# Hybrid attention and recurrence backbone on one core: row maxima over 96 rows, the recurrence's products in fp32, joint logarithms

## The chip, the cores and the metric

One core of one Trainium2 chip runs the whole program in one launch. The metric is device time in microseconds (us), the median of the runs. The engines are TensorE (PE, with its weight loads as PEld), VectorE (DVE), ScalarE (ACT), GpSimd (POOL) and SyncE (SP, which issues the transfers). Each engine takes its own instructions strictly in the order in which the program wrote them.

## The reference, cut to what matters

Two layers over 256 context and 512 latent tokens of width 1024. In each, one in-projection feeds four mixers of four heads (64 wide): A, differential attention; B, a gated recurrence in both directions (HGRN2); C, grouped-query attention; D, a 2-D Fourier transform. An out-projection and a SwiGLU block follow. The change is mostly in B and C:

```python
def forget_gate(z, lb):
    sig = jax.nn.sigmoid(z)
    log_f = jnp.log(lb + (1 - lb) * sig)
    key = (1 - lb) * jax.nn.sigmoid(-z)
    return log_f, key

# B: o_t = sum over s <= t of (q_t . k_s decayed by f between s and t) v_s,
#    forward and backward, latent tokens starting from the context's state
        decay = jnp.where(incl, jnp.exp(rel), 0.0)
        scores = jnp.einsum('bhtd,bhsd,bhtsd->bhts', qc, kc, decay)
        o_intra = jnp.einsum('bhts,bhse->bhte', scores, vc)

# C: 4 query heads on 2 key heads
def gqa_core(q, k, v):
    s = jnp.einsum('bqhgd,bkhd->bhgqk', q.astype(F32), k.astype(F32)) * HEAD_DIM ** -0.5
    p = jax.nn.softmax(s, axis=-1)
    return jnp.einsum('bhgqk,bkhd->bqhgd', p, v.astype(F32)).astype(v.dtype)
```

All inputs are fp32. In layer 0 the gate's lower bound `lb` is zero, so its logarithm has a short form there; layer 1 needs a second logarithm.

## The kernel before, in words

**Tiling.** Tokens are held in three groups g = 0 (context), 1 and 2 (latent), 256 tokens each. A projection multiplies fp16 halves in three passes (high by high, high by low, low by high) into fp32 PSUM; the latent stream's projections are the `MATMUL` lines L2014 and L2019, the FFN's are L2129 (three passes) and L2169, L2233. For most tiles the FFN's first product uses seven products of half-size sums in place of eight (`p_ffn_pair`, L2169); tiles listed in `TUNE['cl']` use plain passes (L2129).

**Order.** The program is written once by `Plan.run`, a list scheduler: each piece of work is a thread with a priority (`pr_...` in `TUNE`) that yields operations with an estimated cost on an engine, or on a choice of two. The plan always writes the operation that can start first by its own estimates. So any changed cost or priority reorders the whole program, and the order it writes is fixed on the chip.

**Mixer C.** `a_prep`/`c_prep` normalise, rotate and split q and k into fp16 halves. Keys are laid out as 192 rows of two tiles `kt[:, 0]` (128 rows) and `kt[:, 1]` (96 rows); `tr` fills them with transposes of 128 and of 64 columns (L1339, L1340). `c_att` first wants each query's largest score, before the score product itself: for each head j and key group it runs a 128-row product (L1376, high and low half of q) and a 64-row product (L1377, high half of q by low half of k), and takes the maximum over the two banks. The maximum then becomes two rows (64 and 65) of a 96-row tile `s2`, which holds the high half of q in rows 0 to 63; its transpose gives `qt[0:96, 1]`, and the score product (L1404, L1405: 128 rows, then 96) subtracts the maximum on the way. `score_thread` follows with exponentials (L1192) and their fp16 halves `ph` and `pl`, the latter by a DVE or POOL subtraction (L424), for A and C alike.

**Mixer B.** `b_gate` and `b_gates` turn gate columns into logarithms: per token group, three `Ln` (L1468) that need another ACT table than the `Exp` around them. `b_levels` forms the decayed scores by doubling: block widths 0, 1, 2, 4 up to 128, with a decay tile E at each (`b_decay`, products at L1605, L1638, L1674), then multiplies scores by values: `b_split` copies a score bank as fp16 high half and subtracts it for the low half (L1553, DVE), and `b_pv` runs `mm3`, three fp16 products of 64 columns (L1514), four times per bank. `b_v` makes the fp16 halves of the values, the low one at L1508. `b_join` does the pairs of latent groups 1 and 2 (fp32 products over 64 rows, L1774), one row half r of a head pair at a time; `b_state` and the products at L1804 bring in the context's state.

Two lines on which much rests:

```python
for n, (i, j) in enumerate(((0, 0), (0, 1), (1, 0))):
    T.matmul(o, lhsT=A[i], rhs=B[j], start=(start and n == 0), stop=(stop and n == 2), skip_group_check=True)
```

Of the kernel before, what the change touches and what calls it, by code (L numbers as in the profile page):

```python
# [97 lines left out]
class Plan:  # L98
# [5 lines left out]
    def __init__(self):  # L104
        self.eng = {}
# [180 lines left out]
def op(eng, cost, reads, writes, fn, port=False):  # L286
    return ("op", ((eng, cost, fn, 0.0, port),), reads, writes)
# [26 lines left out]
def c_act(n, ap=0):  # L314
    return 0.065 + n * 0.833e-3 + 0.093 * ap
# [16 lines left out]
def kernel(ctx: ExitStack, tc: tile.TileContext, xg, wall, wmod, pk32, pk16, dftx, dftc, out):  # L332
# [34 lines left out]
    nhalf = const.tile([128, 16], F32, name="nhalf")  # L367
    vA = [const.tile([128, 2, 4, 2, 65], F16, name=f"vA{g}") for g in range(NG)]
# [21 lines left out]
    st = {}  # L390
# [5 lines left out]
    def aop(cost, r, w, f):  # L396
        return op("act", cost, r, w, f)
# [277 lines left out]
    def prep_thread():  # L675
# [30 lines left out]
        for l in range(NL):  # L706
# [11 lines left out]
            yield vop(0.8, ["cst", "pk32b"], [("lam", l)], f2)  # L718
# [59 lines left out]
    def norm_thread(l, w, g):  # L778
# [1782 lines left out]
```

## Time and profile before

| what | value |
|---|---|
| median of 3 runs | 1769.31 us (1768.81 to 1769.59) |
| profiled execution, its own time | 1768.02 us |
| its span, first to last instruction | 1766.2 us |
| PE busy in the span | 1690.3 us, 96% |
| DVE busy | 1505.1 us, 85% |
| ACT busy | 999.1 us, 57% |
| POOL busy | 142.5 us, 8% |
| mean granted PE clock | 0.975 of full |

The profile is of one execution. A share of busy time is a mean over stages with different limits, so the stages are read apart: in-projection and mixers of layer 0 lie at about 100 to 521 us of the span, its FFN at 521 to 1030, the mixers of layer 1 at 1030 to 1408, its FFN at 1408 to 1766. A PE that is busy all through a stage sets its length; where PE has gaps and DVE has none, DVE does. Matmuls overlap, so the duration of one is not its price: the price is the distance between the starts of neighbours, and is read from the timeline.

### The profile page before, as it was taken

The numbers are of one execution on the slowest core, as the hardware profiler recorded it, in microseconds if no ns is written. First come the engines' busy times: TensorE is split into PE (matmuls) and PEld (weight loads), VectorE is DVE, ScalarE is ACT, GpSimd is POOL, SyncE is SP. The second block draws the span as 40 slices with busy tenths as digits, with TensorE's granted clock in tenths as the row PEclk, the third lists the DMA queues.
The fourth block names the chain that finished last, engine by engine and source line by source line (L and its number), as shares of the span: only waits on it lengthen the run. The fifth ranks groups of instructions, "written<-read, shape, count | busy, mean of one in ns | idle before, by whom it ended". The sixth has DMA issues, their size and how long they took to land. (4 is left out here: it accounts for less than half of the span.)

```text
span 1766.2 us, 46475 instructions
## 1 busy us (share of the span) xinstructions
PE 1690.3 (96%) x19913; PEld 1439.0 (81%) x19913; DVE 1505.1 (85%) x3182; ACT 999.1 (57%) x1816; POOL 142.5 (8%) x166
## 2 busy tenths in 40 slices
PE   8999988899999999999999999999779999999998
PEld 6687877577788889999899888868668888887887
DVE  6888799788569888899889997988999678888887
ACT  5647876465456554355435484539768555465454
POOL 0122021120000000000000002311011000000000
PEclk9999999699999999999999999999979999999999
DMA  9822010145234653521354151000124323452531
GB/s 375 319 83 85 26 57 27 49 132 204 73 132 133 213 170 112 182 81 59 119 179 129 44 180 49 26 25 18 34 73 145 107 83 105 126 185 79 178 122 49
DMA packets 62863, 201.47 MB, mean 114 GB/s; under 512 B 6848, under 2 KB 9152, under 8 KB 62656
## 3 DMA queue, kind: packets, MB, share of 16 engines
q1 hardware_dynamic: 62656, 198.50, 33.6%
q8 instruction: 156, 2.56, 0.6%
q14 instruction: 51, 0.42, 0.1%
HBM read 178.55 MB, written 19.92 MB: 112 GB/s over the span
## 5 line engine op out<-in xcount | busy, mean ns | idle before, releaser
L424 DVE TENSOR_TENSOR g<-g,g 128x512 f32<-128x512 f32 (+6 forms) x705 | 444.3, 654 | 60.5 <-ACT g L410 43.8
L412 ACT ACTIVATE g<-g 128x512 f16<-128x512 f32 (+2 forms) x397 | 243.8, 639 | 247.1 <-DVE g L424 244.6
L2169 PE MATMUL ps<-g,g 128*128 128x256 f16 (+1 forms) x4200 | 374.9, 251 | 0.1
L2169 PEld LDWEIGHTS <-g 128*128 128x128 f16 x4200 | 339.0, 98 | 39.3 <-issue 11.1
L428 DVE SCALAR_TENSOR_TENSOR g<-g,g 128x512 f16<-128x512 f32 (+4 forms) x450 | 305.3, 695 | 56.4 <-ACT g L412 53.2
L2014 PE MATMUL ps<-g,g 128*128 128x256 f16 x2256 | 272.2, 274 | 1.0 <-DVE g L428 1.0
L2233 PEld LDWEIGHTS <-g 128*128 128x128 f16 x2709 | 227.4, 98 | 36.6 <-issue 11.0
L2014 PEld LDWEIGHTS <-g 128*128 128x128 f16 x2256 | 219.0, 98 | 31.8 <-issue 1.7
L410 ACT CAST g<-g 128x512 f16<-128x512 f32 (+3 forms) x283 | 170.4, 613 | 111.6 <-DVE g L424 67.9
L2233 PE MATMUL ps<-g,g 128*128 128x256 f16 (+1 forms) x1917 | 214.4, 271 | 10.2 <-ACT g L410 3.7
L2019 PE MATMUL ps<-g,g 128*128 128x256 f16 x1632 | 197.8, 274 | 0.2 <-DVE g L424 0.2
L2019 PEld LDWEIGHTS <-g 128*128 128x128 f16 x1632 | 155.9, 98 | 28.9 <-issue 7.5
L2129 PE MATMUL ps<-g,g 128*128 128x256 f16 x1440 | 159.7, 273 | 0.0
L2129 PEld LDWEIGHTS <-g 128*128 128x128 f16 x1440 | 140.8, 98 | 17.3 <-issue 0.8
L410 ACT COPY g<-ps 128x512 f32<-128x512 f32 (+4 forms) x130 | 74.2, 572 | 114.2 <-PE ps L814 27.1
L1192 ACT ACTIVATE g<-ps 128x512 f32<-128x512 f32 x156 | 91.4, 597 | 32.4 <-PE ps L1226 22.4
L424 DVE TENSOR_TENSOR pl<-g,ph 128x512 f16<-128x512 f32 x130 | 88.7, 693 | 11.3 <-ACT ph L410 10.2
L424 DVE TENSOR_TENSOR g<-g 128x256 f32<-128x256 f32 (+3 forms) x203 | 93.7, 468 | 3.2 <-ACT g L748 1.8
L410 ACT CAST ph<-g 128x512 f16<-128x512 f32 (+2 forms) x149 | 84.9, 576 | 4.2 <-DVE g L424 1.4
L2427 PE MATMUL ps<-p16c 128*128 128x256 f16 x590 | 75.1, 282 | 3.8 <-DMA p16c<-in_pk_dram 3.8
L2427 PEld LDWEIGHTS <-p16c 128*128 128x128 f16 x590 | 58.9, 102 | 16.5 <-issue 4.2
L1212 PEld LDWEIGHTS <-ph 128*128 128x128 f16 x1248 | 65.4, 98 | 5.6 <-issue 3.2
(242 smaller groups left out, 2243.5 us busy)
## 6 DMA issues: line engine op xcount, KB each, us to landing
g<-in_wall_dram SPq DMA_DIRECT2D x180, 512.0 KB, 4.6
g<-in_wmod_dram SPq DMA_DIRECT2D x96, 512.0 KB, 6.6
g<-xsc SPq DMA_DIRECT2D x40, 256.0 KB, 4.9
xsc<-g SPq DMA_DIRECT2D x40, 256.0 KB, 3.0
g<-in_xg_dram SPq DMA_DIRECT2D x12, 512.0 KB, 6.9
g<-in_wall_dram SPq DMA_DIRECT2D x16, 384.0 KB, 3.3
xsc<-g SPq DMA_DIRECT2D x10, 512.0 KB, 2.8
g<-xsc SPq DMA_DIRECT2D x10, 512.0 KB, 5.4
```

What stands on the lines that cost most here:

```text
L410: S.copy(o, i)
L412: S.activation(out=o, in_=i, func=AF.Copy, scale=scale)
L424: return either(r, w, ("dve", c_dve(n), lambda: V.tensor_tensor(**f()), bias, True), ("pool", c_pool(n), lambda: G.tensor_tensor(**f()), 0 ...
L428: return vop(c_dve(n), r, w, lambda: V.scalar_tensor_tensor(**f()), True)
L1192: yield aop(c_act(512), [k], [k + (0,)], lambda pp=pp, bank=bank: S.activation(out=pp, in_=bank, func=AF.Exp, scale=scale))
L1212: T.matmul(bank[:, u, t, :], lhsT=a[:, i, q], rhs=v[:, b, :], start=(n == 0), stop=(n == 6 * nk - 1))
L2014: T.matmul(bank[:, cb, :], lhsT=W[a][:, kw, 128 * cb:128 * cb + 128], rhs=xh[b][:, kx, :], start=(first and n == 0), stop=(last and n == 2 ...
L2019: T.matmul(bank[:, t, :], lhsT=xh[b][:, k, 128 * t:128 * t + 128], rhs=wt[a][:, k, :], start=(first and n == 0), stop=(last and n == 2), s ...
L2129: T.matmul(bank[:, cb, :], lhsT=wt[a][:, k % 4, :], rhs=xh[b][:, k % 4, :], start=(k == 0 and n == 0), stop=(k == 7 and n == 2), skip_grou ...
L2169: T.matmul(into[name], lhsT=wt[:, y, kk, :], rhs=x[:, z, kk, :], start=(name in ("P1", "P6") and kk == 0 and n == 0), stop=(kk == 3 and n ...
L2233: T.matmul(o, lhsT=wt[:, y, j % 4, :], rhs=x[:, z], start=(name in ("P1", "P6") and j == js[0] and n == 0), stop=(j == js[-1] and n == 2), ...
L2427: T.matmul(t[:, 0:256], lhsT=ident16, rhs=p16[:, 128:384], start=True, stop=True)
```

## The change: what it does

1. **Row maxima of C.** The 64-row product becomes a 96-row one, `qt[0:96, 1]` by `kt[0:96, 1]`. For that, the high half of q is copied to `qt[0:64, 1]` straight from the transposes' bank (a new copy, key `cqh`), and rows 64 to 95 are set to zero by POOL first. The maxima are transposed alone afterwards, in a tile of 32 columns that lands on rows 64 to 95.
2. **Key transposes.** The same eight per group, four of 128 columns first and four of 64 columns after them.
3. **B in fp32** in both layers (`'f32': ('B', 'B')`): values, scores and the transposed decay stay fp32. `b_split` is one copy, `b_pv` one fp32 product in place of three fp16 ones, `b_v` one copy; the subtractions at L1553 and L1508 are gone.
4. **Join.** Both row halves of a head pair are one operation; their products alternate between two banks.
5. **Joint logarithms** in layer 0 (`'jg': (1, 0)`): the nine `Ln` of the three groups run in one block.
6. **FFN**: tile 19 of layer 0 uses plain passes.
7. **Planner**: a table load costs 1.3 when the table changes, other costs and the priorities `pr_cp`, `pr_gate`, `pr_catt` and `bfu` change. This reorders everything.

```diff
-TUNE = {... 'pr_cp': 5, 'pr_gate': 8, ... 'pr_catt': 8, ... 'x3': 2, 'cl': ((0, 1), ...), ... 'bfu': 0.6, ...}
+TUNE = {... 'pr_cp': 7, 'pr_gate': 7, ... 'pr_catt': 10, ... 'x3': 2, 'jg': (1, 0), 'f32': ('B', 'B'), 'cl': ((0, 1, 19), ...), ... 'bfu': 0.8, ...}
...
+            tab = best[2][5] if len(best[2]) > 5 else None
+            if tab and tab != self.tab:
+                self.tab = tab
+                cost += 1.3
...
 def c_act(n, ap=0):
-    return 0.065 + n * 0.833e-3 + 0.093 * ap
+    return 0.095 + n * 0.833e-3 + 0.093 * ap
...
-            s2 = yield alloc("g2", [128, 2, 4, 96], F16, 1)
-            st["cq2", l, g] = s2
-            yield gop(0.25, [], [k + ("z",)], lambda: G.memset(s2[:, :, :, 64:96], 0.0))
-            yield vop(c_dve(512, 0.26), [k + (4,)], [k + (6,)], lambda: V.tensor_copy(s2[:, :, :, 0:64], s1[:, :, :, 0:64]), True)
...
+            yield gop(0.46, [], [k + ("z",)], lambda: G.memset(qt[64:96, 1], 0.0))
             yield cpo(1024, [k + (7,)], [("cq1", l, g)], lambda: (d, tb), ps=False, port=False)
+            yield cpo(1024, [k + (7,)], [("cqh", l, g)], lambda: (d1[0:64], tb[0:64]), ps=False, port=False)
...
-                for t in range(2):
-                    for h in range(2):
-                        T.transpose(tb[:, 0, t, h, :], ks[:, t, h, 0:128], ident16)
-                        T.transpose(tb[0:64, 1, t, h, :], ks[:, t, h, 128:192], ident16)
+                for p, c in ((slice(0, 128), slice(0, 128)), (slice(0, 64), slice(128, 192))):
+                    for t in range(2):
+                        for h in range(2):
+                            T.transpose(tb[p, c.start // 128, t, h, :], ks[:, t, h, c], ident16)
...
+        s2 = yield alloc("qm", [128, 2, 4, 32], F16)
+        yield gop(0.3, [], [("cm", l, g, "z")], lambda: G.memset(s2, 0.0))
...
-                        T.matmul(bank[:, u, :], lhsT=qt[0:64, 0, j, q], rhs=kt[0:64, 1, j // 2, :], start=False, stop=True)
+                        T.matmul(bank[:, u, :], lhsT=qt[0:96, 1, j, q], rhs=kt[0:96, 1, j // 2, :], start=False, stop=True)
...
-                    T.transpose(tb[0:96, t, j, :], s2[:, t, j, :], ident16)
+                    T.transpose(tb[64:96, t, j, :], s2[:, t, j, :], ident16, tile_position=(0, 64))
...
-    def b_gates(l, g):
+    def b_gates(l, gs):
...
-            for d in ds:
-                S.activation(out=e[d], in_=e[d], func=AF.Ln, bias=ones32[:, 0:1])
+            for x in every:
+                S.activation(out=e[x], in_=e[x], func=AF.Ln, bias=ones32[:, 0:1])
...
     def b_v(l, g, bank, bkey):
+        if "B" in FULL[l]:
+            yield cpo(512, [bkey], [("bv", l, g)], lambda: (v, bank), IWS)
+            return
...
     def b_pv(Ob, S2, i, tcol, v, sblk, tblk, h, first):
+        if len(S2.shape) == 3:
+            T.matmul(o, lhsT=S2[:, i, tcol], rhs=v[:, sblk, 64 * h:64 * h + 64], start=first, stop=False, skip_group_check=True)
+            return
...
+    def b_tile(l, n):
+        m = 512 // n
+        return alloc("sch", *(([128, n, m], F32) if "B" in FULL[l] else ([128, 2, n, m], F16)))
...
     def b_split(E, X, keyin, k, n):
+        if len(X.shape) == len(E.shape):
+            yield cpo(n, keyin, [k + ("x",)], lambda: (X, E))
+            return
         yield cpo(n, keyin, [k + ("hi",)], lambda: (X[:, 0], E), ps=True)
         yield vop(c_dve(n), [k + ("hi",)], [k + ("x",)], lambda: V.tensor_tensor(out=X[:, 1], in0=E, in1=X[:, 0], op=ALU.subtract))
...
+                            if full:
+                                T.matmul(o, lhsT=KT[:, d, 2 * hp + b, 64 * r:64 * r + 64], rhs=v[:, b, 64 * h:64 * h + 64], start=b == 0, stop=b == 1)
+                                continue
...
-                    def mm(bank=bank, sg=sg, tg=tg, r=r, hp=hp):
-                        p = slice(64 * r, 64 * r + 64)
-                        for sb in range(2):
-                            T.matmul(bank[:, sb, :], lhsT=E[sg][p, 1, hp, 128 * sb:128 * sb + 128], rhs=E[tg][p, 0, hp, :], start=True, stop=True)
+                def mm(banks=banks, sg=sg, tg=tg, hp=hp):
+                    for sb in range(2):
+                        for r in range(2):
+                            p = slice(64 * r, 64 * r + 64)
+                            T.matmul(banks[r][:, sb, :], lhsT=E[sg][p, 1, hp, 128 * sb:128 * sb + 128], rhs=E[tg][p, 0, hp, :], start=True, stop=True)
...
+            gated = st.setdefault(("gated", l), [])
+            gated.append(g)
+            if not TUNE["jg"][l] or len(gated) == NG:
+                plan.spawn(b_gates(l, list(gated)), TUNE["pr_gates"])
+                gated.clear()
```

**Where instructions stand.** In the rows below, `ps_...` is a PSUM bank, `p16c` a table of constants (the identity here), `g_...` a tile in SBUF; line numbers are those of each kernel. PE, key transposes of a latent group in layer 0, before:

```order
L1339 LDWEIGHTS g_4361
L1339 MATMUL ps_4777<-p16c,g_4361 128x128
L1340 LDWEIGHTS g_4361
L1340 MATMUL ps_4777<-p16c,g_4361 64x128
L1339 LDWEIGHTS g_4361
L1339 MATMUL ps_4777<-p16c,g_4361 128x128
```

and the same place in the changed kernel, the end of the wide ones and the start of the narrow ones:

```order
L1344 LDWEIGHTS g_4860
L1344 MATMUL ps_5050<-p16c,g_4860 128x128
L1344 LDWEIGHTS g_4860
L1344 MATMUL ps_5050<-p16c,g_4860 64x128
L1344 LDWEIGHTS g_4860
L1344 MATMUL ps_5050<-p16c,g_4860 64x128
```

Wide and narrow no longer take turns.

PE in the join of layer 0, before: the end of one half's fp16 value products (`g_5431` holds its scores), the two score products of the other half (L1774, into bank `ps_5465`), and the start of its value products:

```order
L1514 LDWEIGHTS g_5431
L1514 MATMUL ps_5157<-g_1173,g_5431 128x64
L1774 MATMUL ps_5465<-g_5429,g_5312 128x256 x2
L1514 LDWEIGHTS g_5466
L1514 MATMUL ps_5157<-g_1173,g_5466 128x64
```

and in the changed kernel: the fp32 value products of two halves, then the next pair's score products (L1808):

```order
L1558 MATMUL ps_4928<-g_1159,g_5232 128x64 x4
L1558 MATMUL ps_4928<-g_1159,g_5280 128x64 x4
L1808 MATMUL ps_5306<-g_5229,g_5101 128x256
L1808 MATMUL ps_5307<-g_5229,g_5101 128x256
L1808 MATMUL ps_5306<-g_5229,g_5101 128x256
L1808 MATMUL ps_5307<-g_5229,g_5101 128x256
```

Four fp32 products stand where twelve fp16 ones and their weight loads stood, and the score products alternate between two banks.

DVE in the same stretch, before: low halves of score banks (L1553) between the last steps of preparing q for C (L1294, L1295):

```order
L1553 TENSOR_TENSOR g_5496<-ps_5346,g_5496 128x512
L1294 TENSOR_TENSOR g_5202<-g_5202,sm_5204 128x256
L1295 TENSOR_TENSOR g_5202<-g_5202,p32c 128x256
L1653 COPY g_5496<-g_5242 32x8x32 x4
L1553 TENSOR_TENSOR g_5491<-ps_5490,g_5491 128x512
L1553 TENSOR_TENSOR g_5513<-ps_5369,g_5513 128x512
```

and in the changed kernel, where one half's scores are copied whole by DVE (L423; the other half's copy stands on ACT), among steps of the levels (L1635) and of C (L1300, L1301):

```order
L1635 COPY_PREDICATED g_4456<-p16c,ps_5224 128x128
L423 COPY g_5280<-ps_5231 128x512
L1635 COPY_PREDICATED g_4456<-p16c,ps_5225 128x128
L1300 TENSOR_TENSOR g_4995<-g_4995,sm_4997 128x512
L1301 TENSOR_TENSOR g_4995<-g_4995,p32c 128x512
```

The subtractions have left DVE's queue.

## Rows read from the trace of the kernel before

**Rows 1.** The page's part 1: busy us, share of the span, instructions.

```profile
PE 1690.3 (96%) x19913; PEld 1439.0 (81%) x19913; DVE 1505.1 (85%) x3182; ACT 999.1 (57%) x1816; POOL 142.5 (8%) x166
```

**Rows 2.** Stretches: from:to, length, busy PE, PEld, DVE, ACT, POOL, granted clock, DMA.

```profile
220.00:340.00 120.00, 99.53 (x2090) 79.16 (x2088) 114.60 (x289) 74.98 (x131) 26.31 (x29) 0.87 0.13 40
340.00:460.00 120.00, 119.14 (x1292) 87.42 (x1292) 93.59 (x183) 73.37 (x124) 13.04 (x14) 0.97 0.45 150
...
1030.00:1220.00 190.00, 188.66 (x1927) 156.00 (x1925) 162.12 (x330) 115.10 (x182) 35.23 (x39) 1.00 0.13 40
1220.00:1345.00 125.00, 99.40 (x1982) 83.08 (x1981) 121.16 (x273) 92.89 (x156) 15.24 (x13) 0.86 0.21 69
```

**Rows 3.** PE's longest wait, 1220 to 1345: its releaser, us, times, longest.

```profile
PE ps L1605 <- DVE g L424: 7.3, 8, 2.6
```

**Rows 4.** A stretch of 10 us at the low clock, columns as in rows 2.

```profile
1290.00:1300.00 10.00, 3.57 (x52) 2.42 (x52) 10.00 (x26) 4.87 (x10) 1.40 (x2) 0.50 0.16 52
```

**Rows 5.** PE's timeline: row maxima of C (start us, us, what).

```profile
375.28 0.27 PE L1376 MATMUL ps<-g,g 128*128 128x256 f16 x1
375.49 0.28 PE L1377 MATMUL ps<-g,g 64*128 64x256 f16 x1
375.70 0.28 PE L1376 MATMUL ps<-g,g 128*128 128x256 f16 x1
```

**Rows 6.** Line L1377: count, shortest, median and longest ns, first and last start.

```profile
L1377 PE MATMUL ps<-g,g x104: 279/280/280, 352.5 to 1189.9; 64*128 64x256 f16 x104
```

**Rows 7.** PE's timeline: fp32 products over two row halves; score product of C; the join.

```profile
273.33 1.16 PE L1674 MATMUL ps<-g 64*128 64x128 f32 x16 [0.32 <-DVE g L424]
...
1319.00 0.27 PE L1404 MATMUL ps<-g,g 128*128 128x256 f16 x1
1319.11 0.27 PE L1405 MATMUL ps<-g,g 96*128 96x256 f16 x1
...
1319.89 1.13 PE L1774 MATMUL ps<-g,g 64*128 64x256 f32 x4
1320.95 0.28 PE L1404 MATMUL ps<-g,g 128*128 128x256 f16 x1
```

**Rows 8.** PE's timeline: the first of eight key transposes, and what follows them.

```profile
1098.74 0.22 PE L1339 MATMUL ps<-p16c,g 128*128 128x128 f16 x1
...
1100.07 1.49 PE L2019 MATMUL ps<-g,g 128*128 128x256 f16 x12
```

**Rows 9.** Groups of instructions, shapes apart: line, op, count, busy us, mean ns.

```profile
L2129 PE MATMUL ps<-g,g 128*128 128x256 f16 x1440 | 159.7, 273 | 0.0
L2169 PE MATMUL ps<-g,g 128*128 128x128 f16 x1680 | 97.9, 219 | 0.0
```

**Rows 10.** PE's timeline: one bank's fp16 value products and what follows.

```profile
1311.63 0.52 PE L1514 MATMUL ps<-g,g 128*128 128x64 f16 x12 [1.08 <-DVE g L1653]
1311.99 1.48 PE L2014 MATMUL ps<-g,g 128*128 128x256 f16 x12
```

**Rows 11.** PE's timeline: 16 fp32 products of 128 columns, and what follows.

```profile
363.21 3.74 PE L1804 MATMUL ps<-g,g 128*128 128x128 f32 x32
366.79 0.27 PE L1376 MATMUL ps<-g,g 128*128 128x256 f16 x1
```

**Rows 12.** PE's timeline: four fp32 products of one column, and what follows.

```profile
10.92 0.95 PE L793 MATMUL ps<-p32c,g 128*128 128x1 f32 x8
11.73 1.47 PE L2427 MATMUL ps<-p16c 128*128 128x256 f16 x12
```

**Rows 13.** PE's timeline, low clock: twelve fp16 products; four fp32 ones.

```profile
319.71 1.12 PE L1514 MATMUL ps<-g,g 128*128 128x64 f16 x12
...
1302.57 2.22 PE L1709 MATMUL ps<-p32c,g 128*128 128x128 f32 x8
```

**Rows 14.** One group of DVE, in 220 to 340 and in 1220 to 1345.

```profile
L1553 DVE TENSOR_TENSOR g<-ps,g 128x512 f16<-128x512 f32 x15 | 10.0, 684 | 1.8 <-ACT g L410 1.7
...
L1553 DVE TENSOR_TENSOR g<-ps,g 128x512 f16<-128x512 f32 x17 | 11.3, 685 | 1.0 <-ACT g L410 0.9
```

More of the change, by code (lines that the diff above doesn't have):

```diff
@@ L1360, in c_att @@
         qt = st["cqT", l, g]
-        s2 = st.pop(("cq2", l, g))
+        yield wait(("cqh", l, g))
         tb = yield alloc("ps", [128, 2, 4, 128], F16, 1)
+        s2 = yield alloc("qm", [128, 2, 4, 32], F16)
+        yield gop(0.3, [], [("cm", l, g, "z")], lambda: G.memset(s2, 0.0))
         for t in range(2):
@@ L1447, in b_gate @@
         plan.free(bank)
-        if l == 0 and d < 2:
+        if d < 2:
             e = r1[:, 0] if d == 0 else r0[:, 0]
@@ L1452, in b_gate @@
         st["bz", l, g, d] = (z, e)
-        yield aop(c_act(512), [k + (0,)], [k + (1,)], lambda: S.activation(out=e, in_=z, func=AF.Exp, scale=-1.0))
-    def b_gates(l, g):
-        ds = (0, 1, 2) if need_q(l, g) else (0, 1)
-        k = ("bgs", l, g)
-        yield wait(*[("bg", l, g, d, 1) for d in ds])
-        r0, r1, q, sg, v = st["bR", l, g]
-        z = {d: st["bz", l, g, d][0] for d in ds}
-        e = {d: st["bz", l, g, d][1] for d in ds}
-        tf = {0: r1[:, 0], 1: r0[:, 0]}
-        tk = {0: r0[:, 1], 1: r1[:, 1]}
+        yield aop(c_act(512), [k + (0,)], [k + (1,)], lambda: S.activation(out=e, in_=z, func=AF.Exp, scale=-1.0), "exp")
@@ new lines, in b_gates @@
+    def b_gates(l, gs):
+        dirs = [(g, d) for g in gs for d in (0, 1)]
+        every = dirs + [(g, 2) for g in gs if need_q(l, g)]
+        k = ("bgs", l, gs[0])
+        yield wait(*[("bg", l, g, d, 1) for g, d in every])
+        z = {(g, d): st["bz", l, g, d][0] for g, d in every}
+        e = {(g, d): st["bz", l, g, d][1] for g, d in every}
+        R = {g: st["bR", l, g] for g in gs}
+        tf = {(g, d): R[g][1 - d][:, 0] for g, d in dirs}
+        tk = {(g, d): R[g][d][:, 1] for g, d in dirs}
@@ L1479, in b_gates @@
+                yield either([k + (0,), "lbt"], [k + (1, x)], ("dve", 0.8, lambda fk=fk: fk(V), 0.0, True))
         if l:
             def ex():
[L1481 to L1483 removed]
+                for x in dirs:
+                    S.activation(out=z[x], in_=e[x], func=AF.Exp, scale=-1.0)
+            yield aop(len(dirs) * c_act(512), [k + (1, x) for x in dirs], [k + (2,)], ex, "exp")
@@ new lines, in b_gates @@
+            for x in dirs:
+                yield vop(c_dve(512, 0.52), [k + (3,)], [("bgate", l, *x)], lambda x=x: V.tensor_scalar(out=tf[x], in0=e[x], scalar1=-1.0, scalar2=None, op0=ALU.mult), True)
+                plan.free(z[x])
+        for x in every[len(dirs):]:
+            yield aop(c_act(512), [k + (0,)], [k + (4, x)], lambda x=x: S.activation(out=e[x], in_=e[x], func=AF.Exp, scale=-1.0), "exp")
+            yield tto(512, [k + (4, x)], [("bgate", l, x[0], 2)], lambda x=x: dict(out=R[x[0]][3], in0=z[x], in1=e[x], op=ALU.mult))
+            plan.free(z[x])
+            plan.free(e[x])
@@ L1615, in b_levels @@
             plan.free(E)
-        sx = yield alloc("g2", [128, 2, 2, 4, 32], F16, 0)
-        k = base + ("sx",)
-        yield cpo(256, [base + (16, "c", r) for r in range(2)], [k + ("hi",)], lambda: (sx[:, 0], sc), ps=False)
-        yield tto(256, [k + ("hi",)], [k + ("x",)], lambda: dict(out=sx[:, 1], in0=sc, in1=sx[:, 0], op=ALU.subtract))
-        plan.free(sc)
+        full = "B" in FULL[l]
+        cpv = 4 * 0.225 if full else 12 * 0.03
+        if full:
+            sx, sxk = sc, [base + (16, "c", r) for r in range(2)]
+        else:
+            sx = yield alloc("g2", [128, 2, 2, 4, 32], F16, 0)
+            k = base + ("sx",)
+            sxk = [k + ("x",)]
+            yield cpo(256, [base + (16, "c", r) for r in range(2)], [k + ("hi",)], lambda: (sx[:, 0], sc), ps=False)
+            yield tto(256, [k + ("hi",)], sxk, lambda: dict(out=sx[:, 1], in0=sc, in1=sx[:, 0], op=ALU.subtract))
+            plan.free(sc)
         banks = []
@@ L1710, in b_state @@
             yield pop(0.44, [k + (d,)], [k + ("t", d)], tr)
-            yield from b_split(tb, KT[:, :, d], [k + ("t", d)], k + ("k", d), 512)
+            yield from b_split(tb, KT[:, d] if full else KT[:, :, d], [k + ("t", d)], k + ("k", d), 512)
             plan.free(tb)
@@ L1725, in mm @@
                             mm3(o, A, B, b == 0, b == 1)
-        yield pop(48 * 0.03, [k + ("k", 0, "x"), k + ("k", 1, "x"), ("bv", l, 0)], [k + ("m",)], mm)
+        yield pop(16 * 0.12 if full else 48 * 0.03, [k + ("k", 0, "x"), k + ("k", 1, "x"), ("bv", l, 0)], [k + ("m",)], mm)
         plan.free(KT)
```

128 lines of the change are left out of this document (61 added, 67 removed).

## The prediction

> **What bounds the kernel now.** I read the whole-span line first [rows 1]: PE is busy 96% of 1766.2 us, DVE 85%, so one would say PE. The table of stretches [rows 2] corrects that. From 340 to 460 and from 1030 to 1220 PE has 0.9 and 1.3 us of gaps: there a microsecond taken from PE is a microsecond of the kernel, and one taken from DVE (93.6 of 120, 162.1 of 190) is nothing. From 220 to 340 and from 1220 to 1345, where B's levels and its join lie, it is the other way: DVE is busy 114.6 of 120 and 121.2 of 125, while PE has gaps of 20.5 and 25.6 us and a granted clock of 0.87 and 0.86. PE's longest wait there is for a DVE result [rows 3], and in a stretch where PE was busy 3.6 of 10 us and DVE all 10, the clock is 0.50, its lower level [rows 4]. So each edit has to be put into its stretch: C's maxima lie in the two PE-bound ones, B mostly in the two DVE-bound ones. Both FFNs and both out-projections are bounded by PE.
>
> **The change part by part.** Prices are distances between starts.
>
> *Maxima.* A 128-row product and its 64-row neighbour start 0.21 us apart, a pair takes 0.42 [rows 5]. A plain product of 256 columns costs 159.7 / 1440 = 0.111 [rows 9], so each pair loses 0.42 - 0.22 = 0.20, twice 0.10 for a change of row count. The score product of C already runs 128 rows and then 96 at 0.11 each [rows 7], so the new pair should cost 0.22. There are 104 pairs [rows 6], all in PE-bound stretches: 104 x 0.20 = -20.8. The copy `cqh` (five, one per block of q) replaces five copies at L1310: 0 on the path, at most 5 x 1.1 (twice ACT's mean instruction, 999.1 / 1816 = 0.55, as it has 1024 columns) = 5.5 if PE waits for all. The zeroing on POOL is a new wait ahead of C's first product, with all later PE work queued behind it; it needs no input and stands early, so 0; if not, 5 x 142.5 / 166 = 4.3.
>
> *Key transposes.* Eight take 1.33 us [rows 8], 0.166 each; without change of width a product of 128 columns costs 97.9 / 1680 = 0.058 [rows 9]. Six groups of eight: 48 x 0.108 = 5.2, less two changes per group that stay (6 x 2 x 0.10 = 1.2): -4.0, of which two thirds, -2.7, in PE-bound stretches.
>
> *Values by scores.* Twelve fp16 products take 0.36 [rows 10]. Four fp32 ones take their place. Each fp32 product leaves two records; 16 of 128 columns take 3.58 [rows 11], 0.224 each. The new ones have 64 columns, and no row shows that: by columns they would cost half, 4 x 0.112 = 0.45; but four fp32 products of one single column take 0.81 [rows 12], 0.20 each, so columns don't set the price below 128. I take 4 x 0.224 = 0.90, +0.54 a group; there are 36 groups, so +19.4 on PE against +3.2 by columns. The Trainium skill has a rule against this edit ("TensorE: Matmul & The Clock Gate", section on weight-path perf modes): the fast weight load is used only with 128 weights that are not FP32. By that rule, and the trace agrees with 0.20 for one column, the sum is the +19.4; without it the +3.2. Some 30 of the 36 groups lie in the DVE-bound stretches, where PE has gaps of 46 us to hold 16.2; the other six are +3.2 on the path. The context's state (`b_state`) goes from 48 fp16 to 16 fp32 products a layer: 48 x 0.03 (0.36 / 12) = 1.4 against 16 x 0.112 to 16 x 0.224, so +0.4 to +2.2 a layer, and I take +2.0 for both.
>
> *Join.* Two products over one row half take 1.06 [rows 7], 32 products 17.0. The levels' products of 128 columns that alternate between row halves take 1.16 for 16 records [rows 7], against 16 x 0.112 = 1.79 one after another, and most of the rest is the tail of the last; so halves overlap, and the join gives back up to half, 8.5. It lies where DVE is the bound: 0 on the path.
>
> *Small ones on PE.* Tile 19: 144 x 0.111 in place of 84 x 0.111 + 84 x 0.058 [rows 9] = +1.8. The maxima's transposes, ten groups of four, now 32 columns wide in a corner of the array, are a form no row shows: 0 if they cost like others, 10 x 2 x 0.10 = 2.0 if each group pays a change both ways; I take +1.0. The Trainium skill ("TensorEngine Tiling (Array Packing)", section "Key Properties") says that changing the tiling mode drains the engine; rows 5 agree with 0.10 a change, and by it the term would be the 2.0.
>
> *DVE.* The subtractions at L1553 cost 10.0 / 15 = 0.667 each [rows 14]: 15 in the first DVE-bound stretch, 17 in the second, and L1508 of the same form three times in each layer: (15 + 3 + 17 + 3) x 0.667 = -25.3. Against that, the changed order puts 7 low halves `pl` on DVE that POOL did before (26 on POOL become 19): 7 x 0.667 = +4.8 at worst, and I count it all. Net -20.5. What is late next is PE, and close: in the first stretch DVE comes to 114.6 - 12 = 103, PE to 99.5 + 8 - 4 = 103.5 of 120 us (half of the 30 groups and of the join), so the saving fits, with nothing to spare.
>
> *Logarithms.* Five fewer table loads and less ACT work: ACT is busy 75 of 120 and 93 of 125 [rows 2] and bounds nothing: 0. But joining the three blocks makes the first levels wait for the last group's gate. In the changed order the first level product of layer 0 is PE's instruction 4612 in place of 4273: 170 products more ahead of it, up to 19 us by 0.111. In layer 1 it stays (25349 for 25354). I take 0, since PE is full before 220 and does that work at some time anyway, and keep +15 as a bound. In layer 1, on the other hand, the order moves C's softmax ahead of the levels: of 36 `pl` subtractions between the levels and the out-projection 12 are left. 24 x 0.667 = 16 us of DVE would leave a DVE-bound stretch for one with 28 us of DVE idle. I take 0 for it and keep it as a rival, since what else moves in is not seen from counts.
>
> *Sum.* PE-bound: -20.8 - 2.7 + 3.2 + 2.0 + 1.8 + 1.0 = -15.5. DVE-bound: -20.5. Together -36.0 on the profiled execution's 1768.0: 1732.0. The median lies 1.3 above that execution, so **1733**. Its own range: the low end with everything cheap (-20.8 - 4.0 + 0.5 for the six groups by columns + 0.8 + 1.8 + 0 - 25.3 = -47): 1722. The high end with six groups at the low clock's price (6 x 1.1 = 6.6), `b_state` 4.4, transposes 2, DVE -16 (where PE takes up the rest) and the levels 15 later: -20.8 - 2.7 + 6.6 + 4.4 + 1.8 + 2 - 16 + 15 = -9.7, 1760.
>
> **The rivals.** *PE becomes the bound of B's stretches, and the DVE time saved is worth nothing.* Then all PE terms count in full and no DVE term: -20.8 - 4.0 + 19.4 - 8.5 + 2.0 + 1.8 + 1.0 = -9.1: 1760. For it: PE's rate there is already held back by the clock. Against: gaps of 46 us.
>
> *The larger gain.* C's softmax of layer 1 really leaves the DVE-bound stretch: -15.5 - 25.3 - 16 = -57: 1713. For it: the order, and DVE's 28 idle us from 1030 to 1220. Against: those are gaps between dependent steps.
>
> *Slower: the fp32 products run at the low clock, on the path.* At the low clock twelve fp16 products take 1.12, four fp32 ones of 128 columns 2.22 [rows 13], +1.10 a group. If all 30 groups in B's stretches run so and are what ends there, DVE's saving is worth nothing: -15.5 - 8.5 + 30 x 1.10 = +9: 1778. It decides from 22 groups on (24.0 / 1.10). For it: 0.86 and 0.87, and the sparse stretches just where the join lies. Against: less DVE work makes the gaps that precede a low clock shorter, not longer.
>
> *The change doesn't do what it says:* 128 rows against 96 still pays, as q's second tile is a different one from the score product's use of it. Then -36 + 20.8: 1754. Rows 7 speak against it plainly.
>
> **How the numbers follow.** Forecast 0.45; PE the bound 0.20; larger gain 0.17; slower 0.12; the maxima unchanged 0.03; same for other reasons 0.03. The range from 1706 to 1764 holds the forecast's own, PE the bound, the larger gain and the unchanged maxima, and leaves the slower case out. 0.2% is 3.5 us, about what a measurement of this kernel can tell from no change. Faster: 0.45 + 0.20 + 0.17 + 0.03 less 0.01 at the edge = 0.84; within 0.2%: 0.04; slower 0.12.
>
> **What would show it.** Maxima: in the changed trace 128-row and 96-row products start 0.11 apart; at 0.21 the first term is gone. Transposes: eight in about 0.7. Values: four fp32 products (eight records) in 0.90 at full clock; at 0.45 six groups give 2.7 back. DVE: busy time between the levels' start and the join's end down by some 10 us a layer, and PE's waits for it shorter; if PE has no gaps left there while DVE does, it was the first rival. A granted clock of under 0.8 in those stretches would speak for the slower case, one over 0.9 against it. The prediction is wrong if the order as a whole moved the path: a stretch outside of 220 to 460 and 1030 to 1345 that changes by over 10 us has no term here.

## The result and the profile after

The changed kernel takes **1723.35 us** (median of 4 runs, 1718.43 to 1724.57) against 1769.06: a ratio of 0.9738 (95% interval 0.9718 to 0.9757), 46 us less. Ratios leave out two executions far above the others of their kernel, 3398.79 us of `e5` and 1784.86 us of B alone. Forecast were 1733 and 36 less. In the profiled executions the span fell from 1766.2 to 1721.1. By the starts of each FFN's first and last product in the traces, it fell as follows:

| stage | before, us | after, us | difference |
|---|---|---|---|
| to the first FFN product of layer 0 | 520.8 | 491.8 | -29.0 |
| from there to layer 0's last FFN product | 508.1 | 509.8 | +1.7 |
| from there to layer 1's first FFN product | 379.1 | 366.3 | -12.8 |
| from there to layer 1's last FFN product | 343.9 | 338.9 | -5.0 |

B's levels and join, from the first level product to the join's last, took 132.8 us in layer 0 and 119.3 in layer 1 before, and take 87.7 and 102.0 now. The new order put other work ahead of them: the levels start 12.5 us later in layer 0 (231.4 for 218.9), and in layer 1 they start 210.2 us after the first FFN's last product in place of 197.2. So the difference of a stage is not that of one edit.

The stretches of the changed kernel, columns as in [rows 2]. B's levels and join lie in 231 to 343 and 1212 to 1320, C's maxima of layer 0 at 337 to 401, those of layer 1 at 1138 to 1189:

```profile
PE 1660.1 (96%) x19718; PEld 1442.3 (84%) x19718; DVE 1484.4 (86%) x3141; ACT 979.6 (57%) x1766; POOL 149.7 (9%) x179
```

```profile
231.00:343.00 112.00, 100.22 (x2132) 85.92 (x2130) 106.63 (x278) 68.04 (x119) 23.21 (x22) 0.97 0.20 62
343.00:492.00 149.00, 146.55 (x1607) 124.06 (x1605) 113.42 (x228) 82.03 (x138) 19.31 (x17) 1.00 0.40 137
...
1212.00:1320.00 108.00, 95.67 (x1758) 82.49 (x1747) 94.93 (x224) 70.39 (x117) 5.46 (x6) 0.97 0.28 90
1320.00:1368.00 48.00, 47.99 (x439) 42.93 (x439) 33.18 (x55) 30.01 (x41) 4.39 (x5) 1.00 0.28 100
```

PE's gaps in B's stretches went from 20.5 and 25.6 us [rows 2] to 11.8 and 12.3, and the granted clock there from 0.87 and 0.86 to 0.97. In the second stretch PE and DVE are now idle about equally, 12.3 and 13.1 us. PE's longest wait there is of the same kind as in [rows 3], but shorter, 4.5 for 7.3 (waits of PE, 1212 to 1320):

```profile
PE ps L1627 <- DVE g L430: 4.5, 6, 1.4
PE ps L1558 <- ACT g L1582: 2.1, 1, 2.1
```

PE's waits ahead of the value products are seen in their groups of both kernels (records, busy us, mean ns, idle time just before and what ended it), first before, then changed:

```profile
L1514 PE MATMUL ps<-g,g 128*128 128x64 f16 x432 | 23.5, 209 | 17.4 <-DVE g L1653 8.4 <-DVE g L1553 7.0 <-ACT g L410 1.7
```

```profile
L1558 PE MATMUL ps<-g,g 128*128 128x64 f32 x288 | 37.7, 284 | 4.2 <-ACT g L1582 2.1 <-DVE g L1681 0.7 <-DVE g L423 0.7
```

Of the 17.4 us of waits before, 7.0 stood directly behind the subtraction at L1553. The waits fell by 13.2 us, and PE's busy time for these products rose by 14.2.

Three prices of the prediction stand in PE's timeline of the changed kernel. Pairs of 128 and 96 rows start 0.11 apart (L1382, L1383; [rows 5]: 0.21):

```profile
337.63 0.27 PE L1382 MATMUL ps<-g,g 128*128 128x256 f16 x1
337.74 0.27 PE L1383 MATMUL ps<-g,g 96*128 96x256 f16 x1
337.85 0.27 PE L1382 MATMUL ps<-g,g 128*128 128x256 f16 x1
```

Eight key transposes (L1344) take 0.67 against 1.33 in [rows 8], and two banks of fp32 value products (L1558, eight products, 16 records) 1.74, so 0.87 a bank, as priced (0.90) and not the 0.45 that their columns would give:

```profile
328.07 0.74 PE L1344 MATMUL ps<-p16c,g 128*128 128x128 f16 x8
328.74 1.48 PE L2049 MATMUL ps<-g,g 128*128 128x256 f16 x12
330.06 1.90 PE L1558 MATMUL ps<-g,g 128*128 128x64 f32 x16
331.80 1.04 PE L1738 MATMUL ps<-p32c,g 128*128 128x128 f32 x8
```

So these unit prices were right. What the runs had to settle is where they are paid.

### The profile page after: what moved, and what is told of

It reads as the page before. It is cut to its first block, busy times and chain, and to the rows that moved or that the text cites. A ratio compares the mean times of both kernels' runs of the same rounds, so it can differ in the third digit from the quotient of the medians.

```text
span 1721.1 us, 45963 instructions
## 1 busy us (share of the span) xinstructions
PE 1660.1 (96%) x19718; PEld 1442.3 (84%) x19718; DVE 1484.4 (86%) x3141; ACT 979.6 (57%) x1766; POOL 149.7 (9%) x179
## 4 chain that ended last, share of the span: by engine, by line
PE 59%; DVE 27%; ACT 6%; DMA 4%; issue 3%; POOL 1%; SPq 0%; DVEq 0%; ACTq 0%; POOLq 0%
PE ps L2208 15%; PE ps L2049 10%; DVE g L430 7%; PE ps L2168 7%; PE ps L2054 6%; PE ps L2272 5%; DVE g L434 4%; PE ps L616 2%; DMA g<-xsc 2%; PE ps L2466 2%; PE ps L1218 2%; DVE pl L430 1%; ACT g L418 1%; PE ps L1158 1%; DVE g L1548 1%
## 5 line engine op out<-in xcount | busy, mean ns | idle before, releaser
L430 DVE TENSOR_TENSOR g<-g,g 128x512 f32<-128x512 f32 (+7 forms) x698 | 439.9, 656 | 46.8 <-ACT g L416 34.4
L2208 PE MATMUL ps<-g,g 128*128 128x256 f16 (+1 forms) x4032 | 361.4, 251 | 0.0
L434 DVE SCALAR_TENSOR_TENSOR g<-g,g 128x512 f16<-128x512 f32 (+4 forms) x442 | 300.4, 696 | 59.0 <-ACT g L418 56.0
L2049 PE MATMUL ps<-g,g 128*128 128x256 f16 x2256 | 271.8, 273 | 1.8 <-DVE g L434 1.5
L2272 PE MATMUL ps<-g,g 128*128 128x256 f16 (+1 forms) x1917 | 211.0, 269 | 8.3 <-DVE g L999 3.6
L416 ACT CAST g<-g 128x512 f16<-128x512 f32 (+3 forms) x269 | 162.5, 615 | 76.3 <-DVE g L430 46.4
L2054 PE MATMUL ps<-g,g 128*128 128x256 f16 x1632 | 198.2, 274 | 0.0
L2168 PE MATMUL ps<-g,g 128*128 128x256 f16 x1584 | 175.7, 273 | 0.0
L416 ACT COPY g<-ps 128x512 f32<-128x512 f32 (+4 forms) x163 | 94.0, 583 | 120.2 <-PE ps L2272 23.7
L430 DVE TENSOR_TENSOR pl<-g,ph 128x512 f16<-128x512 f32 x137 | 93.0, 694 | 7.1 <-ACT ph L416 6.7
L430 DVE TENSOR_TENSOR g<-g 128x256 f32<-128x256 f32 (+3 forms) x197 | 88.9, 460 | 2.4 <-ACT g L754 1.8
L430 POOL TENSOR_TENSOR g<-g,g 128x256 f16<-128x256 f32 (+4 forms) x17 | 23.5, 1385 | 695.0 <-ACT g L416 579.1
L416 ACT CAST ph<-g 128x512 f16<-128x512 f32 (+2 forms) x141 | 80.3, 572 | 4.7 <-DVE g L430 1.0
```

Source lines behind the costliest of these rows:

```text
L416: S.copy(o, i)
L430: return either(r, w, ("dve", c_dve(n), lambda: V.tensor_tensor(**f()), bias, True), ("pool", c_pool(n), lambda: G.tensor_tensor(**f()), 0 ...
L434: return vop(c_dve(n), r, w, lambda: V.scalar_tensor_tensor(**f()), True)
L2049: T.matmul(bank[:, cb, :], lhsT=W[a][:, kw, 128 * cb:128 * cb + 128], rhs=xh[b][:, kx, :], start=(first and n == 0), stop=(last and n == 2 ...
L2054: T.matmul(bank[:, t, :], lhsT=xh[b][:, k, 128 * t:128 * t + 128], rhs=wt[a][:, k, :], start=(first and n == 0), stop=(last and n == 2), s ...
L2168: T.matmul(bank[:, cb, :], lhsT=wt[a][:, k % 4, :], rhs=xh[b][:, k % 4, :], start=(k == 0 and n == 0), stop=(k == 7 and n == 2), skip_grou ...
```

## Experiments

Unless said otherwise, differences are taken between ratios to the kernel before, times 1769. Four kernels (`e1`, `e3`, `e4`, `e5`) and `e12` keep every engine's order of the changed kernel, except for what their edit adds or swaps; the others let the planner write a new order.

**One edit back, same order: 64 rows.**

```diff
-T.matmul(bank[:, u, :], lhsT=qt[0:96, 1, j, q], rhs=kt[0:96, 1, j // 2, :], start=False, stop=True)
+T.matmul(bank[:, u, :], lhsT=qt[0:64, 0, j, q], rhs=kt[0:64, 1, j // 2, :], start=False, stop=True)
```

> The changed kernel, same order of every engine, with the one edit of the row maxima taken back: the second product reads 64 rows again (high half of q from the first tile) and still waits for the copy and the zeroing. My theory (each change of row count costs 0.10 us on a PE that bounds these stretches): 104 x 0.20 = 20.8 longer than the changed kernel, about 1744 us, ratio to before about 0.986, and the pair again 0.42 us apart. Rival (the order or B's edits made these stretches shorter, PE's price there is hidden by waits): less than 8 us longer.

Measured: 1741.41, ratio 0.9846 (0.9817 to 0.9875), so 19 longer: my theory holds. PE's timeline shows the price back at 0.21 a product:

```profile
338.34 0.27 PE L1382 MATMUL ps<-g,g 128*128 128x256 f16 x1
338.54 0.28 PE L1383 MATMUL ps<-g,g 64*128 64x256 f16 x1
338.76 0.28 PE L1382 MATMUL ps<-g,g 128*128 128x256 f16 x1
```

The maxima's term (-20.8) holds in the changed order: in the profiled execution layer 0's first FFN product comes 9.0 later, layer 1's another 11.6.

**DVE's subtractions given back, same order.**

```diff
-yield cpo(n, keyin, [k + ("x",)], lambda: (X, E))
+yield cpo(n, keyin, [k + ("x",)], lambda: (V.tensor_tensor(out=junk..., in0=E, in1=p16..., op=ALU.subtract), (X, E))[1])
 # and the same in b_v
```

> The changed kernel, same order, with 46 subtractions given back to DVE (score or value bank minus a constant tile into a tile nobody reads, of the removed form), each ahead of the copy that replaced it; nobody waits for them. 46 x 0.667 = 30.7 us of DVE work, some 38 of them (25.3 us) in the stretches of B's levels and join. My theory (DVE bounds those stretches): 20 to 25 longer, about 1745. Rival (the new order or PE sets those stretches now): under 10 longer. Rival on the clock (the gain came from the clock, which follows from PE's gaps): 20 or more longer and the granted clock in the stretches of the levels, now 0.97 in both, back under 0.92.

Measured: 1758.85, ratio 0.9944 (0.9925 to 0.9964): 36 longer, more than the 30.7 us of work that was added. The first stretch as above, and the stretch from layer 1's first level product (1231.7) to its join's end (1349.4):

```profile
231.00:343.00 112.00, 91.66 (x1941) 76.66 (x1939) 104.25 (x270) 56.64 (x97) 18.06 (x14) 0.87 0.12 38
...
1232.00:1350.00 118.00, 100.83 (x1682) 84.39 (x1676) 103.64 (x237) 67.55 (x110) 5.25 (x6) 0.87 0.23 73
```

PE, which got no work, has 20.3 us of gaps in the first in place of 11.8, and the clock falls from 0.97 to 0.87, the value before the change. In layer 1 the levels start 20 us later than in the changed kernel and the join ends 36 later (1349.4 for 1313.8); the clock between them is 0.87 as well, where the changed kernel has 0.97 from its first level product to its join's end. The rival on the clock expected just this, in both layers.

One point of the expectation did not come out: something did wait for the subtractions. 35 of the 46 copies behind them, all on ACT, started only when the subtraction of their bank had ended (who waited for the subtractions, us, times):

```profile
  ACT g L416: 57.5, 31
  ACT g L418: 5.7, 4
```

PE's waits ahead of the value products (L1558) rose with it, from 4.2 to 19.1 us:

```profile
L1558 PE MATMUL ps<-g,g 128*128 128x64 f32 x288 | 47.1, 327 | 19.1 <-ACT g L416 10.1 <-DVE g L1681 7.8 <-ACT g L1582 0.9
```

So the run gives back a step between score product and value product as well as work in DVE's queue. The kernel before had such a step too (the low half is subtracted after the high half's copy), but the run doesn't tell the price of the step from that of DVE's time.

**PE's fp32 value products twice, same order.**

```diff
...
 T.matmul(o, lhsT=S2[:, i, tcol], rhs=v[:, sblk, 64 * h:64 * h + 64], start=first, stop=False, skip_group_check=True)
+T.matmul(o, lhsT=zt, rhs=v[:, sblk, 64 * h:64 * h + 64], start=False, stop=False, skip_group_check=True)
```

> The changed kernel, same order, with every fp32 value product followed by one with a tile of zeros as weights (adds nothing): 144 more products, 144 x 0.224 = 32.3 us more of PE. My theory (DVE still bounds B's stretches, PE has gaps of 12 and 12 us there): about 27 us of it fall in them and mostly fill gaps, the rest is paid, 5 to 12 longer. Rival (PE is the bound there now): 25 to 32 longer.

Measured: 1748.08, ratio 0.9886 (0.9863 to 0.9909): 26 longer, 0.81 of the 32.3 us added. My theory falls, the rival holds. The gaps of B's stretches took little of the work in: from 231 to 343 PE was still 7.6 us short of full in place of 11.8, at a full clock, and DVE less busy than before the addition (99.40 for 106.63):

```profile
231.00:343.00 112.00, 104.38 (x2179) 92.13 (x2176) 99.40 (x265) 63.90 (x111) 19.11 (x19) 1.00 0.13 43
```

So a microsecond of subtraction given back costs 1.2 there, and a microsecond more on PE costs 0.8. I read this as one chain in which both stand (score product, copy, value product, and each level's product after DVE's tile), not side by side; the waits above fit it, but no run takes the chain itself apart.

**The join's products by row half, same order.**

```diff
-for sb in range(2):
-    for r in range(2):
+for r in range(2):
+    for sb in range(2):
```

> The changed kernel, same order but for the join's products: the two of one row half first, then the two of the other, so that the halves no longer alternate. My theory (its 8 x 1.06 = 8.5 us of PE lie where DVE is the bound): 0 to 3 longer. Rival (PE bounds the join): 8 to 14 longer, as the join's products took 23.7 us with waits before and take 9.9 now.

Measured: ratio 0.9755 (0.9729 to 0.9782), 3 longer, no difference clear of the noise. Pairing in the join is worth little on the path, as forecast.

**The recurrence back in fp16.** `'f32': ('', '')`.

> The changed kernel with the recurrence back in fp16 halves in both layers, everything else as changed; the plan is made anew. From the two runs before: 46 subtractions given back cost 36 us, and fp32 products are paid at 25 / 32 = 0.77 of their PE price. My theory now: B's fp32 gave 36 on DVE and took (30 x 0.54 + 6 x 0.54 + 2) x 0.77 = 16 on PE, so fp16 is about 20 longer, 1743. Rival (a new plan finds other work for the waits): under 8 longer.

Measured: 1733.97, ratio 0.9799 (0.9772 to 0.9826): 11 longer, between the two. Granted clock 0.984 to 0.987 in its four runs, against 0.994 to 0.996 of the changed kernel.

**Logarithms apart.** `'jg': (0, 0)`.

> The changed kernel with layer 0's logarithms in three blocks again (one per token group), plan made anew. My theory (ACT bounds nothing): within 5 of the changed kernel, four table loads more (5.1 us of ACT) hidden. Rival A (joining them made the levels wait: they start 12.5 us later than before): 8 to 12 shorter. Rival B (the table loads stood on the way to the levels): 5 or more longer.

Measured: 1725.22, ratio 0.9749 (0.9718 to 0.978): no difference. The levels start at 211.7 in place of 231.4, and the first FFN product at 489.7 in place of 491.8. My theory holds as far as a kernel with a new order can tell: no price of the table loads or of the later start is seen.

**The old planner.** Old priorities and costs, logarithms apart, tile 19 as before; C and B as changed.

> The edits of C and B alone under the planner's old numbers: old priorities, costs, no table cost, logarithms apart, tile 19 as before. My theory (the edits make the gain): 1720 to 1732. Rival (the new order makes a good part of it, by moving C's softmax of layer 1 ahead of the levels): 1740 or more.

Measured: 1742.28, ratio 0.9831 (0.9786 to 0.9877). The rival's number, but the four runs are not one value: 1741.45, 1743.11 and 1745.23 at a mean clock of 0.982 or 0.983, and 1729.27 at 0.992, of the same instructions. Where the clock goes in an execution of the first kind (stretches of 10 us):

```profile
300.00:310.00 10.00, 8.75 (x193) 7.51 (x192) 9.78 (x24) 2.92 (x6) 6.67 (x6) 1.00 0.50 146
310.00:320.00 10.00, 6.17 (x58) 5.04 (x59) 7.89 (x22) 5.30 (x10) 3.32 (x5) 0.67 0.04 14
320.00:330.00 10.00, 10.00 (x72) 8.14 (x71) 8.33 (x28) 4.50 (x7) 2.53 (x5) 0.50 0.18 52
330.00:340.00 10.00, 10.00 (x47) 8.91 (x45) 5.63 (x10) 4.39 (x8) 0.53 (x1) 0.50 0.09 14
340.00:350.00 10.00, 10.00 (x73) 8.90 (x73) 2.19 (x5) 2.71 (x5) 0.00 (x0) 0.63 0.10 41
```

PE is sparse around 310 to 320 (6.17 of 10), the clock drops to its lower level there, and stays through 20 us and more in which PE has no gap at all: 10.00 busy, at half the clock. The changed kernel around its join (306 to 319):

```profile
300.00:310.00 10.00, 8.98 (x164) 7.45 (x156) 9.97 (x23) 5.38 (x10) 2.66 (x2) 1.00 0.01 2
310.00:320.00 10.00, 9.96 (x135) 8.23 (x134) 9.72 (x30) 6.62 (x12) 2.23 (x4) 1.00 0.01 2
320.00:330.00 10.00, 9.33 (x81) 8.10 (x81) 8.74 (x27) 4.79 (x7) 1.98 (x4) 0.83 0.35 106
```

**A nudge of the planner**, one cost by 0.001, in the changed kernel and in the one before.

```diff
-    return 0.095 + n * 0.833e-3 + 0.093 * ap
+    return 0.096 + n * 0.833e-3 + 0.093 * ap
```

> The changed kernel with one cost of the planner nudged, an ACT instruction's fixed part 0.096 in place of 0.095: nothing but the order changes. My theory: within 5 of the changed kernel. Rival (the order is a lottery of its own and single edits can't be told from it): 8 or more either way, which would widen what the re-planned runs can tell.

> The kernel before with the same nudge of the planner as the changed kernel had in e9, 0.066 in place of 0.065: only the order changes. Theory that the edits make the gain, with the order a spread of about 15 on either: 1755 to 1785. Rival (the kernel before had an unlucky order, and a good part of the 45 us is luck): 1750 or less.

Measured: 1738.78, ratio 0.983 (0.9797 to 0.9862), 16 longer than the changed kernel, so my theory falls and the rival holds; and 1777.76, ratio 1.006 (1.0039 to 1.0082), 11 longer than the one before. The first one's loss lies in layer 0 alone: its first FFN product starts at 506.4 for 491.8. So the order by itself was worth 16 and 11 us in these two draws, and what a re-planned kernel says of a single edit is no finer than that. The kernel before had no unlucky order by this one draw.

**C's edits alone, and B's edits alone, in the kernel before.**

> The kernel before with C's edits alone (96 rows, the new copy, narrow transposes of the maxima, key transposes by width); B and the planner as before; the plan is made anew, as the copies differ. Theory (the 0.20 per pair is paid in full): 104 x 0.20 + 2.7 - 2 = 21 shorter than before, 1748, give or take the order's 15. Rival (it was worth less in the order of before): 1760 or more.

> The kernel before with B's edits alone (fp32 values, scores and state, join by pairs), C as before, planner's numbers as before. Together with C alone (2 shorter than before), both under the old planner (27 shorter) and the changed kernel with B in fp16 (35 shorter) it fills the square. Theory (B is worth 36 on DVE less 16 on PE by the runs of frozen order): 20 shorter, about 1749, give or take the order's 15. Rival (C's saving only counts where B's edits stand, so that B alone brings nearly all of both): 1742 or less. Rival (the fp32 products' price on PE eats the saving without the new order): 1762 or more.

Measured for C: 1767.64, ratio 0.999 (0.9981 to 1.0), 2 shorter: the theory falls, the rival holds. The 0.20 per pair is there (layer 0's first FFN product at 510.5 for 520.8, and layer 1's levels start 8.5 sooner after the first FFN), but in layer 1 the time from the first level product to the join's last went from 119 to 146 us. The new order put 36 of the `pl` subtractions there, in place of 25 (DVE's group of each kernel: the one before in 1226 to 1345, then C alone in 1211 to 1357, then the changed kernel in 1212 to 1313), and at its start ACT is full and PE sparse at a low clock:

```profile
L424 DVE TENSOR_TENSOR pl<-g,ph 128x512 f16<-128x512 f32 x25 | 17.1, 685 | 0.4 <-ACT ph L410 0.3
```

```profile
L424 DVE TENSOR_TENSOR pl<-g,ph 128x512 f16<-128x512 f32 x36 | 24.8, 700 | 1.1 <-ACT ph L410 1.1
```

```profile
L430 DVE TENSOR_TENSOR pl<-g,ph 128x512 f16<-128x512 f32 x13 | 8.8, 683 | 0.0
```

```profile
1211.00:1221.00 10.00, 3.24 (x148) 2.71 (x148) 6.03 (x16) 9.95 (x17) 0.97 (x1) 0.67 0.34 107
1221.00:1231.00 10.00, 8.16 (x148) 6.91 (x149) 7.03 (x18) 9.95 (x14) 0.31 (x1) 0.65 0.01 2
```

Measured for B: ratio 1.0015 (0.9981 to 1.0048), no difference; the theory of 20 falls, and by the median the second rival holds. But the executions are again of two kinds. Three at a mean clock of 0.988 or 0.989 took 1757.45, 1757.97 and 1761.26, some 10 shorter than before; six at 0.974 to 0.976 took 1774.95 to 1779.92, some 9 longer. The instructions and their order are the same, so the 18 us between the kinds go with the clock; what sets the kind is not shown.

The square: C alone 2 shorter, B alone 0, both under the old planner 30. Together they gave far more than the sum of each alone. Whether that is the edits or the order's spread (11 and 16 us in the two draws above), no run tells.

**Wide transposes of the maxima, same order.**

```diff
-s2 = yield alloc("qm", [128, 2, 4, 32], F16)
+s2 = yield alloc("qm", [128, 2, 4, 96], F16)
...
-T.transpose(tb[64:96, t, j, :], s2[:, t, j, :], ident16, tile_position=(0, 64))
+T.transpose(tb[0:96, t, j, :], s2[:, t, j, :], ident16)
```

> The changed kernel, same order, but the maxima's tile is 96 columns wide again (zeros but for two columns), so its 40 transposes have the plain form; only the target rows 64 to 95 are copied on. In the changed kernel's trace the 40 narrow ones take 5.8 us where the wide ones took 2.4 before, each group's first start 0.16 late. My theory (each group pays a change of the array's form on a PE that bounds the stretch): 2 to 3.4 shorter than the changed kernel, 1720. Rival (waits for the maxima hide it, and a longer zeroing on POOL delays the first maxima): 0 to 3 longer.

Measured: 1723.73, ratio 0.9744 (0.9727 to 0.9761), no difference; the theory falls, the rival holds. The 40 narrow transposes are busy 4.0 us, the wide ones here 3.9. What I had read as a price of the corner form was a wait for DVE's maxima (2.5 us in the one, 2.7 in the other). No run beat the changed kernel.

## Why the prediction was right, and where not

**Direction and range held. The reading of B's stretches, as bound by DVE with PE's gaps as room, did not.** By its steps:

- *Maxima, -20.8:* 19 by the run of frozen order. Right in mechanism and size there; in the order of before, C's edits gave 2. *Key transposes, tile 19:* 0.67 for eight, while their worth on the path (-2.7) was not measured; the first FFN is 1.7 longer, +1.8 forecast. *Join:* 3, not clear of noise, right as 0. *Logarithms:* 0, right as far as a new order can tell; the table loads fell from 26 to 22, four and not five, and the levels did start 12.5 us later, inside the bound of 15. In layer 1 I read an unchanged instruction number as an unchanged start; the levels start 13.0 later after the first FFN there, as the value products counted ahead of that number had become fewer. *`b_state`:* its fp32 products are busy 2.4 us where the 96 fp16 ones were 2.1, so +0.3 and not +2.0. *Narrow transposes:* 0, not +1.0. By the Trainium skill ("TensorEngine Tiling (Array Packing)", section "Key Properties") a change of tiling mode drains the engine; for this form the run shows no price, so the 2.0 by that rule falls.
- *DVE, -20.5: the step that was mis-sized.* The 46 operations are worth 36. Two errors are in it. I counted 38 of them into B's stretches; and I gave them their duration as time on a busy engine, though those on score banks also stood between a score product and its value products, and they act on the clock as well. The clock's part can be estimated from B alone: between its two kinds the mean clock differs by 0.0135, at two levels 1 and 0.5 this is 2.7% of the span or 48 us less at the low level, and the time differs by 18, so 0.38 us per us at the low level. The old planner's two kinds give 0.42 (14.0 us for 33.6), and a line through the 42 runs of the kernel before (0.973 to 0.978) 0.38. With the subtractions back the mean clock falls from 0.995 to 0.982, 46 us more at the low level: an estimate of 18 of the 36. The other 18 are the step and the work themselves, and PE's waits ahead of the value products grew by 14.9 us in that trace.
- *fp32 value products, +3.2 of +19.4 paid: the step that failed.* I took PE's gaps in B's stretches for room. The doubled products were paid at 0.81, so the edit cost some 0.81 x 19.4 = 16. By the reading above, the gaps are waits in a chain in which PE's own products stand, and work put into it makes it longer.
- *The clock had no term in the sum.* It stood among the rivals, priced only as a loss. By the same 0.38, the kernel before spent 4.8% of its span at the low level (0.976 in the middle of its runs; 85 us) and the changed one 1% (17 us): 68 x 0.38 = 26 us of the 46. That is an estimate, from the slopes of three kernels.

With these the account comes to -19 maxima, -2.7 transposes, -18 DVE's work, +16 fp32 on PE, +1.8 tile 19, -26 clock, together -48 for 46 measured. That it comes so close is partly luck, since the order's own spread, 11 and 16 us in two draws, has no term in it. My sum was right to 10 us since it left out a gain (the clock, some 26) and a cost (13 more for the fp32 products) that offset each other in part. The same account fits the fp16 run: 33 us more at the low level (0.9855 for 0.995) is +13, and 18 of DVE's work back against 16 of PE's saved is +2: +15 for 11 measured, within the order's spread. **By these estimates B in fp32 is about even on the path alone, and in the changed order it pays by keeping PE's gaps short and its clock up.** That is worked out from two runs of frozen order and a slope, and agrees with the waits of the traces (13.2 us less of them for 14.2 more of PE); it wasn't measured in one run. It is no rule for other orders: with B alone under the old planner most executions stood at 0.974 to 0.976, no higher than the kernel before, and were no faster.

The first rival, PE as the bound of B's stretches, had PE's price right (0.81 paid) and DVE's wrong (36, not nothing). The larger gain came in part: in layer 1's stretch the new order left 13 `pl` subtractions of 25, 8.3 us less on DVE where I had 16. The account leaves this out, as it does the order's other moves. The slower case didn't come: the clock rose, as the argument against it said. That the edit does nothing is excluded by 0.11 in place of 0.21. Outside of the stretches with a term, layer 1's FFN is 5.0 shorter; its order is new and a stretch of low clock in it is gone, but no run tells more.

**Open:** how much of the 46 is the planner's part. Under the old one the two edits gave 42 us in the execution at 0.992 and 26 to 30 in the others (against 1771.10, the kernel before beside them), and a nudge of 0.001 moved a kernel by 11 and by 16. Why C and B give next to nothing alone and 30 together is open as well. Why the same instructions sometimes keep the clock and sometimes not (B alone three times, the old planner once) stays open too.

## What to carry to other kernels

Where two engines hand work to each other in turn, gaps of one are no room for more work on it: test both sides with the order frozen before hiding a cost there. Read the mean granted clock of every run beside its time: a saving on DVE that closes PE's gaps may pay twice, and an order that opens one gap may lose 14 us, as the old planner's executions did. Where a scheduler writes the program, nudge it once without a reason; the spread that this gives is a first error bar of every single edit.

## What the runs showed of the hardware

- A drop to the low clock outlasts the gap that precedes it: in the old planner's run PE was busy 10.00 of 10 us at 0.50 in two stretches on end. Identical instructions (B alone) ran 18 us apart at mean clocks of 0.988 and 0.975.
- An fp32 product's price is about the same for 1, 64 and 128 moving columns (0.20, 0.22, 0.22 us) with 128 weights; with 64 weights it is far less, 32 products (64 records) in 2.4 us busy (L1753).
- Changing between 128 and 64 rows costs 0.10 us each way (starts 0.21 apart), between 128 and 96 rows nothing (0.11 apart, as a plain product).
